# Expert layer of a float32 network: products with the weights' low parts moved to the end of each block, gates transposed together, and the context's first norm moved into the sums over V

## Chip, cores and metric

The kernel runs on one core of one Trainium2 chip. The metric is the time of one execution in microseconds of device time. The time before is 4041.46 us (the median of three runs). The profile below is of one more execution of the same program.

## What is computed

The network (d_model 1024, 512 tokens and a context of 256 tokens, all float32) has a first block of mixers, an expert layer, and a second block that works on the tokens together with the context. The change lies in the expert layer and where it meets the second block:

```python
def peer_ffn(xn, w_q, sub_keys, expert_u, expert_v):
    qh = (x2 @ w_q).reshape(t, PEER_HEADS, 2, PEER_QDIM // 2)
    scores = jnp.einsum('thcd,hckd->thck', qh, sub_keys, ...)
    sv, si = lax.top_k(scores, PEER_TOPK)
    ...
    cv, ci = lax.top_k(cand.reshape(...), PEER_TOPK)
    experts = (i1 * PEER_NKEYS + i2).reshape(t, PEER_HEADS * PEER_TOPK)
    gates = jax.nn.softmax(cv, axis=-1).reshape(...)
    # each token, for its 128 experts out of 16384:
    act = jax.nn.gelu(einsum('tkd,td->tk', expert_u[eb], xb))
    return einsum('tk,tkd->td', act * gb, expert_v[eb])
```

## The kernel before

**Float32 products.** A float32 operand is split into a high part and the rest (`split`, and `wload` for weights). `wload` loads 128x1024 raw weights (`wr`, three buffers, L194), ACT copies the high part `wh` (L142), and DVE subtracts to get the low part `wl` (L199). `mm3` then issues three matmuls for one product: L204 high by high, L205 and L206 with one low part each. `tt` is DVE's two-operand operation (L145), `stt` its operation with a scalar in between (L148), `copy` ACT's copy (L142), `transpose` a matmul with the identity (L236).

**The expert layer** (`peer`) treats the first 128 tokens apart from the other 384. For the 384, all 16384 experts are computed densely. `peer_h` makes H = gelu(U x) in 128 blocks of 128 experts, with 8 `mm3` (24 matmuls with 384 columns) to a block. In H, L204 and L205 use `wh` (L205 with x's low part) and L206 uses `wl`. A pair of blocks is written to the DRAM tensor `Hd` (L976). `peer_select` (on DVE) finds the 128 experts of each token, makes their gates and transposes both into three tiles `pi` (copies at L892 and L908). `peer_g` makes from them, by comparison with `iota` (`oa`, `ob`, then `ob` scaled by ACT) and 96 groups of 4 products (L995, 8 matmul records in the trace), a matrix G of gates which is zero wherever a token did not choose an expert, and writes it to `Gd` (L999). `peer_v` then sums over V. For each of its 128 blocks it needs V's block (`wh`, `wl`), H times G (`pa`, loaded as a pair of blocks from `Hd` at L1120 into one of two buffers, multiplied in place by `pg`, the loaded G, L1114) and the split of that product (`ph` by ACT, `pl` by DVE). A block is 18 matmuls with 512 columns into six accumulators. In V, L204 is ph by vh, L205 ph by vl (which needs `wl`), L206 pl by vh (which needs `pl`), three by three.

**The sparse path** handles the other 128 tokens: POOL gathers each token's rows of U (L915) and DVE takes the dot products (L931). In V's time POOL gathers rows of V, and PE sums them in groups of 8 small matmuls (L956, weights `sw`).

**Behind V** the sums are copied out (`py`, L1146), transposed (L236) and added to x; the squares of x are summed (`nsq`, `na`), and a matmul with ones (L267) begins x's norm. The stage `ctx0` starts with the context's norm (`norm`: for each of 8 slices `nt` on DVE, `xh` on ACT, `xl` on DVE, all 128x256) and projections of the context, 24 matmuls with 256 columns each; beside them a table of modulations is made (`mods`, L1175, weights `mw` from `wmod`).

**What sets the order.** Each engine executes its queue in order. The queues are what the scheduler of the tile framework makes of the program's order and of its own estimates, and the program's order comes from `interleave`, which runs several generators as lanes; each `yield busy, gap` tells it how far that lane's clock moves. H is the spare lane during selection and G, so where it yields decides where the other lanes' work may come between. A transfer is issued from SP's queue, in order too.

Of the kernel before, what the change touches and what calls it, by code (L numbers as in the profile page):

```python
# [23 lines left out]
CTX = 256  # L24
# [8 lines left out]
TS = 128  # L33
TD = SEQ - TS
# [8 lines left out]
def flat(t):  # L43
    return t.rearrange("p a b -> p (a b)")
# [61 lines left out]
class Net:  # L106
# [95 lines left out]
    def mm3(s, out, ah, al, bh, bl, start, stop):  # L202
        mm = s.nc.tensor.matmul
        mm(out, ah, bh, start=start, stop=False)  # L204
        mm(out, ah, bl, start=False, stop=False)  # L205
        mm(out, al, bh, start=False, stop=stop)  # L206

    def proj(s, w, xh, xl, nk, T, k0=0):

# [617 lines left out]
    def peer_select(s, p, sc, iota, iT, S):  # L827


        nc = s.nc  # L830
        cvs, late = [], []
        for tt in range(4):
# [60 lines left out]
                                          b[:, c * 128:(c + 1) * 128])  # L893
            late.append(transposed)
        late.pop(0)()
        for tt in range(4):
            ge = S["ge"] if tt == 0 else s.t(p, "pge", [128, 8, 16], 2)
            gm = s.t(p, "pgm", [128, 16], 2)[:, :8]
            s.tt(ge, cvs[tt], cvs[tt][:, :, 0:1].to_broadcast([128, 8, 16]), ALU.subtract)
            s.act(ge, ge, AF.Exp)  # L900
            yield 0.0, 1.0
            nc.vector.tensor_reduce(gm, ge, axis=AX.X, op=ALU.add)
            nc.vector.reciprocal(gm, gm)
            s.tt(ge, ge, gm[:, :, None].to_broadcast([128, 8, 16]), ALU.mult)
            if tt:
                b = s.bank()
                s.transpose(b[:, 0:128], flat(ge))
                nc.vector.tensor_copy(iT[2][:, (tt - 1) * 128:tt * 128], b[:, 0:128])  # L908
        S["gated"] = True

    def gather(s, S, table, idx):
# [50 lines left out]
    def peer_h(s, hp, xh, xl, Hd):  # L962

        for j in range(128):
            w = s.w()
            s.prime(min(2, 127 - j))
            ps = s.accb()[:, :TD]
            for k in range(8):
                s.mm3(ps, w[0][:, k, :], w[1][:, k, :], xh[:, k, TS:], xl[:, k, TS:], k == 0, k == 7)
                if k == 3:  # L970
                    yield 2.1, 0.0
            if j % 2 == 0:
                h = s.t(hp, "h", [128, 2, TD], 2)
            s.act(h[:, j % 2], ps, AF.Gelu_apprx_tanh)
            if j % 2:
                s.nc.sync.dma_start(Hd[j // 2], h)  # L976
            yield 2.1, 0.0
# [23 lines left out]
    def peer(s, x):  # L1001

        nc = s.nc
        with ExitStack() as st:
            dp = s.pool(st, "pd", space=bass.MemoryType.DRAM)
            Hd = dp.tile([64, 128, 2, TD], F32, name="Hd")
            Gd = dp.tile([TD // 32, 128, 128, 32], F32, name="Gd")
            keep = dp.tile([128, 8, SEQ], F32, name="keepx")  # L1010
            sp = s.pool(st, "sp")
            S = dict(n=0, rows=s.t(sp, "rows", [128, 128], 1, U32), rowsT=s.t(sp, "rowsT", [128, 128], 1, U32),
                     ge=s.t(sp, "sge", [128, 8, 16], 1), act=s.t(sp, "sact", [128, 128], 1),
                     aT=s.t(sp, "saT", [128, 128], 1), xt=s.t(sp, "sxt", [128, DM], 1),
                     w=[s.t(sp, f"sw{n}", [128, 4, 64], 1) for n in range(3)],
                     ring=[flat(x[:, 2 * n:2 * n + 2, :]) for n in range(4)]
                     + [s.t(sp, f"sr{n}", [128, DM], 1) for n in range(2)])
            for w in S["w"]:
                nc.gpsimd.memset(w, 0.0)
            v0 = s.pool(st, "pv0")  # L1020
            with ExitStack() as t:
                sv = s.peer_hg(t, x, Hd, Gd, S, keep)
            s.peer_v(v0, s.pool(st, "pv1"), x, Hd, Gd, S, sv, keep)

    def peer_hg(s, st, x, Hd, Gd, S, keep):
# [75 lines left out]
    def peer_v(s, p0, p1, x, Hd, Gd, S, sv, keep):  # L1101
# [8 lines left out]
        def dense():  # L1110
            js = 0
            for E in [2] + [6] * 21:
                g = s.t(p0 if js == 0 else p1, "pg", [128, TD // 32, E, 32], 1 if js == 0 else 2)
                nc.sync.dma_start(g, Gd[:, :, js:js + E, :].rearrange("b p j t -> p b j t"))  # L1114
                for e in range(E):
                    p, n = (p0, 2) if js % 4 < 2 else (p1, 2)
                    vh, vl = s.wload(s.I["V"][js], 8, p, n)
                    if js % 2 == 0:
                        a = s.t(p0 if js == 0 else p1, "pa", [128, 2, TD], 1 if js == 0 else 2)
                        nc.sync.dma_start(a, Hd[js // 2])  # L1120
                    av = a[:, js % 2].rearrange("p (b t) -> p b t", t=32)
                    s.tt(av, av, g[:, :, e, :], ALU.mult)
                    ah, al = s.t(p, "ph", [128, TD], n, F32R), s.t(p, "pl", [128, TD], n, F32R)
                    s.split(ah, al, a[:, js % 2])
                    vh, vl = flat(vh), flat(vl)
                    for h in range(2):
                        hh = slice(512 * h, 512 * h + 512)
                        for t in range(3):
                            tt = slice(128 * t, 128 * t + 128)
                            s.mm3(acc[t][h], ah[:, tt], al[:, tt], vh[:, hh], vl[:, hh], js == 0, js == 127)  # L1130
                    js += 1
                    yield 4.1, 0.0
            assert js == 128
# [3 lines left out]
            for k in range(8):  # L1137
                nc.sync.dma_start(x[:, k, :], keep[:, k, :])

        interleave([sv, reload(), dense()])  # L1140
        y = s.t(p1, "py", [128, 4, DM], 1)
        for h in range(2):
            hh = slice(512 * h, 512 * h + 512)
# [586 lines left out]
    def block2(s, x):  # L1730
# [3 lines left out]
        with ExitStack() as st:  # L1734
# [10 lines left out]
            xs, xf = [], []  # L1745
            with ExitStack() as t:
                s.mark("ctx0")
                xc, np_ = s.pool(t, "xc"), s.pool(t, "np")
                gain = s.small(np_, "nfin", 8)
                nc.sync.dma_start(gain, s.I["nfin"])  # L1750
                s.layer_consts(np_, 0)
                ch = s.norm(np_, xc, cx, mc[0][:, 8:16], CTX, mc[0][:, 0:8], s.early_r)
                with ExitStack() as t2:
                    s.mixers(t2, 0, CTX, xc, *ch, cx, True, [s.x_entry(np_, x, gain, xp, mx[0], xs),
                                                                    s.mods(s.pool(t2, "md"), 1, 0.5, 4)])
                mx.append(s.mod[1, 0])
                mc.append(s.mod[1, 1])
                for k in range(8):
                    nc.sync.dma_start(cx[:, k, :], s.I["ctxT"][:, k, :])
                s.mark("wo0c")  # L1760
                s.wo(np_, cx, CTX, mc[0], s.y)
                s.early_r = s.rstd(s.early, CTX)
            for i in range(2):
                if i:
                    s.mark("ctx1")
# [192 lines left out]
def network(st, tc, I):  # L1958
    s = Net(st, tc, I)
    s.mark("norm")  # L1960
    s.setup()
    x = s.pool(st, "xres").tile([128, 8, SEQ], F32, name="x")
    s.block1_mix(x)
    s.early = s.pool(st, "early")
    s.peer(x)
    s.block2(x)

# [17 lines left out]
```

## Time and profile before

| | us |
|---|---|
| runs shown: median, lowest, highest of 3 | 4041.46, 4036.75, 4047.43 |
| profiled execution: its own time | 4043.52 |
| profiled execution: span in the trace | 4041.8 |
| PE busy over the span | 3909.7 (97%) |
| DVE busy over the span | 2282.9 (56%) |
| ACT busy over the span | 1679.0 (42%) |
| granted TensorE clock, mean | 0.988 |

Times in the rows are microseconds from the start of the span. The stages that the change touches follow each other: selection with H beside it (about 790 to 1165), the rest of H with G (1165 to 1537), V (1537 to 2198), and the passage into `ctx0` (2198 to about 2220). A row of the view by stretch gives, per engine, busy time and the count of instructions. A row of a group gives busy time and mean duration, and behind the bar the time that the engine sat idle just before these instructions, with what ended it. PEld is the load of weights into TensorE, which overlaps the matmuls.

### The profile page before, as it was taken

What the parts mean: (1) busy time and instruction counts of PE and PEld (TensorE: products, weight loads), DVE (VectorE), ACT (ScalarE), POOL (GpSimd) and SP (SyncE); (2) the same over time, 40 slices, a digit from 0 to 9 for tenths busy, and PEclk for the clock granted to TensorE, in tenths of its full rate; (3) what the DMA queues carried; (4) which work ended last, traced back from release to release, by engine and by line L of the source; (5) the groups of instructions that cost most, each with busy time, mean ns of one, the idle gap of its engine ahead of it and who ended that gap; (6) DMA issues with size and microseconds to landing.
All of it is one profiled execution on the core that took longest, in us unless ns stands there. A gap on an engine that the chain in (4) does not pass through costs nothing.

```text
span 4041.8 us, 58180 instructions
## 1 busy us (share of the span) xinstructions
PE 3909.7 (97%) x22509; PEld 3272.3 (81%) x22509; DVE 2282.9 (56%) x4845; ACT 1679.0 (42%) x3136; POOL 328.0 (8%) x287
## 2 busy tenths in 40 slices
PE   8999999999999999999998999989999999989998
PEld 5878988789999995676777877878888888868887
DVE  7527544559999953344446847673222266664334
ACT  5335444433338872233333645552121245553222
POOL 0000000003234402322200000000000000000000
PEclk9999999999999999999999999999999999999999
DMA  5342123338789968888874751222212131122332
GB/s 196 106 151 77 34 92 106 114 109 282 255 278 367 382 221 310 279 299 291 293 273 162 253 200 48 67 65 68 63 63 65 58 128 63 48 89 80 98 94 84
DMA packets 218596, 637.63 MB, mean 158 GB/s; under 512 B 25552, under 2 KB 65360, under 8 KB 214736
## 3 DMA queue, kind: packets, MB, share of 16 engines
q1 hardware_dynamic: 181456, 499.69, 36.5%
q0 software_dynamic: 36864, 134.23, 9.1%
q8 instruction: 177, 2.90, 0.3%
q14 instruction: 99, 0.81, 0.1%
HBM read 575.12 MB, written 58.72 MB: 157 GB/s over the span
## 4 chain that ended last, share of the span: by engine, by line
PE 75%; DVE 13%; DMA 7%; issue 3%; ACT 2%; POOL 0%; SPq 0%; DVEq 0%; ACTq 0%; POOLq 0%
PE ac L204 18%; PE ac L205 18%; PE ac L206 18%; DMA pa<-Hd 6%; DVE wl L199 4%; PE bk L236 3%; PE bk L995 2%; PE po L1360 2%; PE bk L1175 1%; PE bk L204 1%; PE bk L205 1%; PE bk L206 1%; PE bk L561 1%; PE bk L555 1%; DVE pl L145 1%
## 5 line engine op out<-in xcount | busy, mean ns | idle before, releaser
L204 PE MATMUL ac<-xh,wh 128*128 128x512 f32 (+2 forms) x3608 | 1296.7, 361 | 12.9 <-ACT xh L142 4.4
L206 PE MATMUL ac<-xh,wl 128*128 128x512 f32 (+2 forms) x3608 | 1278.5, 355 | 6.1 <-DVE wl L199 5.8
L205 PE MATMUL ac<-xl,wh 128*128 128x512 f32 (+2 forms) x3608 | 1278.3, 355 | 0.8 <-DVE xl L148 0.6
L142 ACT ACTIVATE wh<-wr 128x1024 fp32r<-128x1024 f32 (+1 forms) x599 | 629.8, 1053 | 1555.7 <-PE ac L205 1109.3
L199 DVE TENSOR_TENSOR wl<-wr,wh 128x1024 fp32r<-128x1024 f32 (+1 forms) x599 | 727.6, 1216 | 558.6 <-ACT wh L142 520.6
L204 PEld LDWEIGHTS ac<-xh,wh 128*128 128x128 f32 x3608 | 682.2, 190 | 105.7 <-issue 17.0
L206 PEld LDWEIGHTS ac<-xh,wl 128*128 128x128 f32 x3608 | 681.9, 189 | 91.1 <-DVE wl L199 12.2
L205 PEld LDWEIGHTS ac<-xl,wh 128*128 128x128 f32 x3608 | 682.8, 190 | 78.3 <-issue 6.7
L145 DVE TENSOR_TENSOR pa<-pa,pg 128x384 f32<-128x384 f32 x128 | 66.2, 556 | 302.3 <-DMA pa<-Hd 291.0
L204 PE MATMUL bk<-wh,ph 128*128 128x512 f32 x512 | 202.0, 394 | 0.0
L206 PE MATMUL bk<-wh,pl 128*128 128x512 f32 x512 | 201.4, 393 | 0.0
L205 PE MATMUL bk<-wl,ph 128*128 128x512 f32 x512 | 201.2, 393 | 0.0
L204 PE MATMUL ac<-ah,wh 128*128 128x512 f32 (+1 forms) x528 | 186.1, 352 | 0.0
L205 PE MATMUL ac<-al,wh 128*128 128x512 f32 (+1 forms) x528 | 185.4, 351 | 0.0
L206 PE MATMUL ac<-ah,wl 128*128 128x512 f32 (+1 forms) x528 | 185.2, 351 | 0.0
L915 POOL DMA_INDIRECT x<-Ur,rows x86 | 123.2, 1433 | 399.5 <-DVE sc L825 212.4
L148 DVE SCALAR_TENSOR_TENSOR x<-ac,mod,x 128x512 f32<-128x512 f32 (+1 forms) x64 | 46.4, 726 | 188.2 <-PE ac L206 187.9
L142 ACT ACTIVATE ob<-ob,pi 128x128 f32<-128x128 f32 x384 | 125.1, 393 | 30.4 <-DVE ob L145 30.3
L142 ACT ACTIVATE ph<-pa 128x384 fp32r<-128x384 f32 x128 | 66.6, 521 | 169.1 <-issue 63.2
L915 POOL DMA_INDIRECT x<-V,rowsT x86 | 92.1, 1071 | 386.1 <-PE bk L956 363.0
L145 DVE TENSOR_TENSOR nt<-ac,nt 128x512 f32<-128x512 f32 (+1 forms) x44 | 29.9, 680 | 160.1 <-PE ac L206 159.8
L205 PE MATMUL ac<-wl,ph 128*128 128x512 f32 x256 | 103.5, 404 | 17.0 <-DVE wl L199 16.9
(453 smaller groups left out, 5843.1 us busy)
## 6 DMA issues: line engine op xcount, KB each, us to landing
wr<-win SPq DMA_DIRECT2D x151, 512.0 KB
wr<-U SPq DMA_DIRECT2D x128, 512.0 KB
wr<-V SPq DMA_DIRECT2D x128, 512.0 KB
mw<-wmod SPq DMA_DIRECT2D x96, 512.0 KB
Hd<-h SPq DMA_DIRECT2D x64, 384.0 KB
pa<-Hd SPq DMA_DIRECT2D x64, 384.0 KB
Gd<-gs SPq DMA_DIRECT2D x24, 1024.0 KB
pg<-Gd SPq DMA_DIRECT2D x21, 1152.0 KB
```

The source lines that it names most:

```text
L142: s.nc.scalar.activation(out, in_, AF.Copy, **kw)
L145: s.nc.vector.tensor_tensor(out, a, b, op=op)
L148: s.nc.vector.scalar_tensor_tensor(out, a, sc, b, op0=op0, op1=op1)
L199: (eng or nc.vector).tensor_tensor(lo[:, :nk, :], raw[:, :nk, :], r32(hi[:, :nk, :]), op=ALU.subtract)
L204: mm(out, ah, bh, start=start, stop=False)
L205: mm(out, ah, bl, start=False, stop=False)
L206: mm(out, al, bh, start=False, stop=stop)
L236: s.nc.tensor.transpose(out, in_, s.ident)
L555: mm(b[:, j], off[:, j], mi[:, j], start=True, stop=True)
L915: s.nc.gpsimd.indirect_dma_start(out=g, out_offset=None, in_=table, in_offset=bass.IndirectOffsetOnAxis(ap=idx, axis=0))
L995: nc.tensor.matmul(b[:, i * 128:(i + 1) * 128], a1[:, i], a2[:, i], start=True, stop=True)
L1360: mm(out[64 * h:64 * h + 64], heads[h][4][j], pt[:, 2 * (j - j0) + h, :], start=False, stop=j == nb - 1, skip_group_check=True)
```

## The change

1. A new `mm3s` for H issues the 16 products with `wh` of a block first and its 8 with `wl` behind them. The yield in the middle of a block moves behind the block.
2. In V a block's 18 products come as 6 ph·vh, 6 pl·vh, 6 ph·vl.
3. The gates of the three dense token blocks are kept in `pix` buffers; after all four are made the lane yields, then three transposes go into one bank and one 128x384 copy takes them out.
4. The context's first norm is a lane of V's `interleave` and its results lie in the pool `xc`, opened ahead of V on the right side of the memory, and closed behind the context's output projection.
5. `ctx_stack` is the stack that holds this pool.

```diff
+    def mm3s(s, out, w, xs, start=True, stop=True):
+        mm = s.nc.tensor.matmul
+        n = len(xs)
+        for k, (xh, xl) in enumerate(xs):
+            mm(out, w[0][:, k, :], xh, start=start and k == 0, stop=False)
+            mm(out, w[0][:, k, :], xl, start=False, stop=False)
+        for k, (xh, _) in enumerate(xs):
+            mm(out, w[1][:, k, :], xh, start=False, stop=stop and k == n - 1)
...
+        ges = []
         for tt in range(4):
-            ge = S["ge"] if tt == 0 else s.t(p, "pge", [128, 8, 16], 2)
+            ge = S["ge"] if tt == 0 else s.t(p, "pix", [128, 8, 16], 4)
             gm = s.t(p, "pgm", [128, 16], 2)[:, :8]
+            ges.append(ge)
...
-            if tt:
-                b = s.bank()
-                s.transpose(b[:, 0:128], flat(ge))
-                nc.vector.tensor_copy(iT[2][:, (tt - 1) * 128:tt * 128], b[:, 0:128])
+        yield 0.0, 6.0
+        b = s.bank()
+        for tt in range(1, 4):
+            s.transpose(b[:, (tt - 1) * 128:tt * 128], flat(ges[tt]))
+        nc.vector.tensor_copy(iT[2], b[:, :TD])
...
-            for k in range(8):
-                s.mm3(ps, w[0][:, k, :], w[1][:, k, :], xh[:, k, TS:], xl[:, k, TS:], k == 0, k == 7)
-                if k == 3:
-                    yield 2.1, 0.0
+            s.mm3s(ps, w, [(xh[:, k, TS:], xl[:, k, TS:]) for k in range(8)])
+            yield 2.1, 0.0
...
+            s.xc = s.ctx_stack.enter_context(s.tc.tile_pool(name="xc", bufs=1, side="right"))
             s.peer_v(v0, s.pool(st, "pv1"), x, Hd, Gd, S, sv, keep)
...
-                    for h in range(2):
-                        hh = slice(512 * h, 512 * h + 512)
-                        for t in range(3):
-                            tt = slice(128 * t, 128 * t + 128)
-                            s.mm3(acc[t][h], ah[:, tt], al[:, tt], vh[:, hh], vl[:, hh], js == 0, js == 127)
+                    for a_, v_, part in ((ah, vh, 0), (al, vh, 1), (ah, vl, 2)):
+                        for h in range(2):
+                            for t in range(3):
+                                nc.tensor.matmul(acc[t][h], a_[:, 128 * t:128 * t + 128],
+                                                 v_[:, 512 * h:512 * h + 512], start=js == 0 and part == 0,
+                                                 stop=js == 127 and part == 2)
...
-        interleave([sv, reload(), dense()])
+        s.ch, mc = [], s.mod[0, 1]
+        interleave([sv, reload(), s.norm_lane(p1, s.xc, s.cx, mc[:, 8:16], CTX, mc[:, 0:8], s.early_r, s.ch), dense()])
...
-                xc, np_ = s.pool(t, "xc"), s.pool(t, "np")
+                np_ = s.pool(t, "np")
...
-                ch = s.norm(np_, xc, cx, mc[0][:, 8:16], CTX, mc[0][:, 0:8], s.early_r)
...
-                    s.mixers(t2, 0, CTX, xc, *ch, cx, True, [s.x_entry(np_, x, gain, xp, mx[0], xs),
+                    s.mixers(t2, 0, CTX, s.xc, *s.ch, cx, True, [s.x_entry(np_, x, gain, xp, mx[0], xs),
```

The scheduler makes new queues of this. DVE's queue in the middle of V, first before (`pa` in place is the product with the loaded G, one row for both blocks of a pair; the blocks' `pl` and `wl` follow it):

```order
L145 TENSOR_TENSOR pa_15631<-pa_15631,pg_15490 128x384 x2
L145 TENSOR_TENSOR pl_15562<-pa_15558,ph_15561 128x384
L199 TENSOR_TENSOR wl_15555<-wr_15552,wh_15554 128x1024
L145 TENSOR_TENSOR pl_15591<-pa_15558,ph_15590 128x384
L199 TENSOR_TENSOR wl_15586<-wr_15583,wh_15585 128x1024
L953 COPY sw_1172_6418<-saT_6416 128x4
L145 TENSOR_TENSOR pa_15693<-pa_15693,pg_15685 128x384 x2
```

and in the change:

```order
L145 TENSOR_TENSOR pa_15994<-pa_15994,pg_15926 128x384
L199 TENSOR_TENSOR wl_15962<-wr_15959,wh_15961 128x1024
L145 TENSOR_TENSOR pl_15967<-pa_15934,ph_15966 128x384
L199 TENSOR_TENSOR wl_15991<-wr_15988,wh_15990 128x1024
L145 TENSOR_TENSOR pl_15998<-pa_15994,ph_15997 128x384
L145 TENSOR_TENSOR pa_16067<-pa_16067,pg_15926 128x384 x2
L199 TENSOR_TENSOR wl_16022<-wr_16019,wh_16021 128x1024
L145 TENSOR_TENSOR pl_16027<-pa_15994,ph_16026 128x384
```

Before, `pl` and `wl` of both blocks of a pair (here of `pa_15558`) stand behind the next pair's `pa` (`pa_15631`). In the change those of the pair's first block (`wl_15991`, `pl_15998` of `pa_15994`) stand ahead of the next pair's `pa_16067`, and only those of the second block behind it.

PE's queue behind V, first before (`py` are the sums, `na` the squares of x, `xh` and `xl` the context's normed parts, of which the first projection takes 24 matmuls):

```order
L236 MATMUL bk_18268<-ident,py_18215 128x128 x4
L236 MATMUL bk_18277<-ident,py_18215 128x128 x4
L236 MATMUL bk_18286<-ident,py_18215 128x128 x4
L267 MATMUL bk_18393<-na_18230,ones 128x512
L204 MATMUL ac_18424<-xh_18350,wh_13982 128x256
L205 MATMUL ac_18424<-xl_18351,wh_13982 128x256
```

and in the change (`L247` and `L278` are the former L236 and L267; between the two pieces lie two projections of 24 matmuls each):

```order
L247 MATMUL bk_18301<-ident,py_18248 128x128 x4
L204 MATMUL ac_18420<-xh_14010,wh_13981 128x256
L205 MATMUL ac_18420<-xl_14011,wh_13981 128x256
L247 MATMUL bk_18310<-ident,py_18248 128x128 x4
L206 MATMUL ac_18420<-xh_14010,wl_13982 128x256
L247 MATMUL bk_18319<-ident,py_18248 128x128 x4
...
L206 MATMUL ac_18459<-xh_14010,wl_13988 128x256
L278 MATMUL bk_18389<-na_18263,ones 128x512
L204 MATMUL ac_18501<-xh_14010,wh_18455 128x256
```

The two projections that followed the matmul with ones now precede it; behind it come two further ones and then the table of modulations. In DVE's queue two `wl` of these projections now stand between the last sums of `na`.

SP's queue at the end of H, first before (`wr<-U` are the loads of H's last blocks):

```order
L999 DMA Gd<-gs_13390 128x2048
L976 DMA Hd<-h_13578 128x768
L999 DMA Gd<-gs_13390 128x2048
L194 DMA wr_13752<-U 128x1024
L194 DMA wr_13980<-win 128x1024
L1114 DMA pg_14011<-Gd 128x12x64
```

and in the change:

```order
L194 DMA wr_13748<-U 128x1024
L194 DMA wr_13979<-win 128x1024
L988 DMA Hd<-h_13644 128x768
L1011 DMA Gd<-gs_13456 128x2048 x2
L194 DMA wr_13985<-win 128x1024
L1128 DMA pg_14016<-Gd 128x12x64
```

The last write of G stands behind the last load of U and the load of the next weights instead of ahead of them, so nearer to the end of H. On PE the last group of G stands two and a half blocks of H later, and G's groups come two at a time behind a whole block instead of one behind each half.

## Rows read from the trace of the kernel before

**Rows 1.** The page, the chain that ended last: shares by line.
```profile
PE ac L204 18%; PE ac L205 18%; PE ac L206 18%; DMA pa<-Hd 6%; DVE wl L199 4%; PE bk L236 3%; PE bk L995 2%; PE po L1360 2%; PE bk L1175 1%; PE bk L204 1%; PE bk L205 1%; PE bk L206 1%; PE bk L561 1%; PE bk L555 1%; DVE pl L145 1%
```

**Rows 2.** By stretch: length, busy PE, PEld, DVE, ACT, POOL; clock, DMA share, GB/s.
```profile
930.00:1165.00 235.00, 224.53 (x1250) 217.95 (x1248) 228.18 (x761) 74.35 (x103) 77.78 (x54) 0.99 0.83 277
...
1280.00:1400.00 120.00, 120.00 (x803) 120.00 (x802) 119.95 (x188) 96.26 (x241) 63.18 (x44) 1.00 1.00 396
...
1710.00:2062.00 352.00, 336.90 (x1576) 250.50 (x1568) 152.28 (x230) 109.90 (x143) 73.33 (x70) 0.99 0.81 293
...
2197.00:2210.00 13.00, 6.24 (x40) 4.89 (x38) 12.04 (x22) 6.48 (x11) 0.00 (x0) 0.81 0.02 2
```

**Rows 3.** Groups, 1710 to 2062: busy, mean ns, idle before, releaser.
```profile
L205 PE MATMUL ac<-wl,ph 128*128 128x512 f32 x144 | 58.3, 405 | 15.1 <-DVE wl L199 15.1
...
L145 DVE TENSOR_TENSOR pa<-pa,pg 128x384 f32<-128x384 f32 x71 | 36.6, 556 | 199.7 <-DMA pa<-Hd 192.7 <-issue 7.1
...
L205 PEld LDWEIGHTS ac<-wl,ph 128*128 128x128 f32 x144 | 27.3, 189 | 25.0 <-DVE wl L199 20.2
```

**Rows 4.** DVE and PE in order of time, one pair of V: start, duration, idle before.
```profile
1767.14 1.03 DVE L145 TENSOR_TENSOR pa<-pa,pg 128x384 f32<-128x384 f32 x2 [10.21 <-DMA pa<-Hd]
1768.09 0.55 DVE L145 TENSOR_TENSOR pl<-pa,ph 128x384 fp32r<-128x384 f32 x1
1768.55 1.22 DVE L199 TENSOR_TENSOR wl<-wr,wh 128x1024 fp32r<-128x1024 f32 x1
...
1769.83 0.50 PE L205 MATMUL ac<-wl,ph 128*128 128x512 f32 x1 [2.26 <-DVE wl L199]
...
1777.25 1.03 DVE L145 TENSOR_TENSOR pa<-pa,pg 128x384 f32<-128x384 f32 x2 [5.87 <-DMA pa<-Hd]
```

**Rows 5.** SP in the same stretch: the pair's load.
```profile
1770.27 0.33 SPq L1120 DMA_DIRECT2D pa<-Hd  x1
```

**Rows 6.** PE in order of time, from V's last product into `ctx0`.
```profile
2197.91 3.65 PE L236 MATMUL bk<-ident,py 128*128 128x128 f32 x32
2208.32 2.04 PE L267 MATMUL bk<-na,ones 128*128 128x512 f32 x2 [6.76 <-DVE na L145]
2209.38 1.20 PE L204 MATMUL ac<-xh,wh 128*128 128x256 f32 x1
...
2217.80 0.28 PE L206 MATMUL ac<-xh,wl 128*128 128x256 f32 x1
2219.11 0.39 PE L204 MATMUL ac<-xh,wh 128*128 128x256 f32 x1 [1.03 <-ACT za L1512]
```

**Rows 7.** The context's norm in its place of before: one of its two DVE groups.
```profile
L148 DVE SCALAR_TENSOR_TENSOR nt<-cx,mod,nr 128x256 f32<-128x256 f32 x8 | 3.5, 480 | 0.0
```

**Rows 8.** The chain of waits at V's start: the second pair's load.
```profile
1543.73 17.99 DMA pa<-Hd
```

**Rows 9.** Waits of an engine for another, 790 to 1165: us, times, longest.
```profile
PEld ac L206 <- DVE wl L199: 8.3, 15, 1.9
```

**Rows 10.** Groups, 1165 to 1524: the scaling of `ob`, and G's weights.
```profile
L142 ACT ACTIVATE ob<-ob,pi 128x128 f32<-128x128 f32 x384 | 125.1, 393 | 30.4 <-DVE ob L145 30.3
...
L995 PEld LDWEIGHTS bk<-ob,oa 128*128 128x128 f32 x768 | 100.7, 191 | 0.9 <-ACT ob L142 0.7
```

**Rows 11.** PE just behind a group of G, in order of time: H's products.
```profile
1284.78 0.42 PE L204 MATMUL ac<-xh,wh 128*128 128x384 f32 x1
1285.04 0.34 PE L205 MATMUL ac<-xl,wh 128*128 128x384 f32 x1
1285.21 0.34 PE L206 MATMUL ac<-xh,wl 128*128 128x384 f32 x1
```

**Rows 12.** SP, DVE and PE from G's last write to V's first product, in order of time.
```profile
1513.46 0.45 SPq L999 DMA_DIRECT2D Gd<-gs  x1
...
1524.45 0.56 DVE L145 TENSOR_TENSOR pa<-pa,pg 128x384 f32<-128x384 f32 x1 [2.11 <-DMA pg<-Gd]
...
1536.74 0.48 PE L204 MATMUL ac<-wh,ph 128*128 128x512 f32 x1
```

More of the change, by code (lines that the diff above doesn't have):

```diff
@@ L1762, in block2 @@
                 s.early_r = s.rstd(s.early, CTX)
+            s.ctx_stack.close()
             for i in range(2):
@@ L1963, in network @@
     s.block1_mix(x)
-    s.early = s.pool(st, "early")
+    s.early, s.ctx_stack = s.pool(st, "early"), st.enter_context(ExitStack())
     s.peer(x)
```

## The prediction

> **What bounds the kernel now.** I read the chain of waits first [rows 1]: PE's three products of the split arithmetic hold 54% of the span between them, and one transfer, the load of `pa`, another 6%. So the kernel is bound by PE nearly throughout, and an edit can gain only where PE stands still. Next I read busy times by stretch to see where that is [rows 2]. In 930 to 1165 (selection beside H) PE is busy for 224.53 of 235 us, and DVE for 228.18: two engines share the bound there. In 1280 to 1400 (H with G) both are full, 120.00 and 119.95 of 120. In the middle of V, 1710 to 2062, PE is busy for 336.90 of 352 us and DVE for only 152.28. Behind V, 2197 to 2210, PE works for 6.24 of 13 us, at a granted clock of 0.81 between its levels of 1.2 and 2.4 GHz, while DVE works for 12.04. Third, the groups of 1710 to 2062 tell what PE's 15.1 idle us there wait for: all 15.1 stand at L205 in the first accumulators, for `wl` [rows 3]. DVE is not short of time there. It sat 199.7 us in front of `pa`, and 192.7 of that ended with the load of `pa`.
>
> The order in time shows how these belong together [rows 4]. DVE takes its queue in order, so the `wl` of a block stands behind the next pair's `pa`: the wait for the load (10.21 us) ends at 1767.14, then come two `pa`, a `pl`, and only at 1768.55 the `wl`, 1.22 us long. PE's L205 starts at 1769.83 after a wait of 2.26, though the raw weights had nothing to do with `pa`. The next load leaves SP at 1770.27, when the pair's `pl` have freed a buffer [rows 5], and `pa` is used at 1777.25, 6.98 us later [rows 4]. That is a loop: 3.1 us of DVE, then a load. By the count of pairs in the stretch it takes 352 / 36 = 9.8 us a pair, while PE's work is 336.90 / 36 = 9.4.
>
> **The change, part by part.**
>
> *V's products, and what DVE's new queue makes of them.* Now PE needs `wl` at the second product of a block; in the change it needs `pl` at the seventh and `wl` at the thirteenth. The queue moves too: `wl` and `pl` of a pair's first block stand ahead of the next pair's `pa` in about three pairs of four (in the fourth, half of the `pa` comes first), and only the second block's stay behind it. So a late load no longer stops the first block. For the second block its `wl` ends 1.03 + 1.22 = 2.3 us behind the start of `pa` and is wanted twelve products in, over 2 us after the block began. The number of products, weight loads and vector operations stays the same. The gain lies between nothing (the loop of 3.1 us and a load stays the bound, and what PE no longer waits for at L205 it waits for at the start of a block) and 25 us (PE's weight loads sat idle for 25.0 us at that place, which takes in what pipelined ends hide [rows 3]). I take three quarters of PE's 15.1: **-11 us**. What is late next is `ph` of the next pair, since it needs the load itself.
>
> *The passage into ctx0.* Now the transposes (begun 2197.91, 3.65 us) end at about 2201.6; PE waits 6.76 us for DVE's last sum of squares, runs the matmul with ones at 2208.32, and two projections of 48 products from 2209.38 to 2217.80, on parts that DVE and ACT make at the same time [rows 6]. In the change these two projections have their operands long before and run among and behind the transposes. At the 8.4 us that they took, slow start and waits included, they end at about 2210. DVE gets two `wl`, 2 x 1.22 = 2.4 us [rows 4], between the last sums, so the matmul with ones comes at 2208.32 + 2.4 = 2210.8 and its duration to the next matmul is 2209.38 - 2208.32 = 1.1. PE is then at 2211.9 where it was at 2217.9 before, so 6.0 us are gained; of the 1.03 us that it stood before the third projection I expect the rest, as its weights are ready. **-7 us**, between 0 (the modulation table's loads, which cannot start earlier, take the time back) and -10 (6.76 + 1.03 + the slow clock's part).
>
> *The norm in its new place.* It is 16 DVE operations of about 0.48 us, 7.7 us by the row [rows 7], and 8 on ACT. They come ahead of the second pair's `pa`, whose load lasts 17.99 us at V's start [rows 8], with DVE idle for most of it and PE busy with the sparse sums: **0**. Without that cover it would delay the first `pa` products by up to 7.7 us, once.
>
> *H and selection.* The products with `wl` come 16 products into a block, not 3. PE's weight loads waited 8.3 us for `wl` in 790 to 1165 [rows 9]. But DVE is 97% busy in most of that, and none of its work goes except two small copies of gates; what PE gains it meets again where it waits for selection's results. **-3 us**, between -8 and +5 (G's start now waits for one copy of all gates).
>
> *G's groups in pairs.* A change from G to H costs PE one slow step: 1284.78 to 1285.04 is 0.26 us against 0.17 for the next [rows 11]. With 48 changes instead of 96, 48 x 0.09 = 4.3 us at most; half of it, as DVE is full there as well: **-2 us**.
>
> *G's last write.* It stood at 1513.46; the loaded G was used at 1524.45 and V's first product ran at 1536.74 [rows 12]. The last group of G moves back by two and a half blocks of H, each 24 products at 0.17, so 24 x 0.17 x 2.5 = 10.2 us. That puts the first `pa` at 1534.7, then `ph`, so just ahead of V's first product: **+1 us**, between 0 and +6.
>
> The **sum** is -11 - 7 - 3 - 2 + 1 = -22 us. The profiled execution took 4043.52 us, 1.7 over its span, and lies 2.1 above the median of the runs shown; on that median it gives 4041.46 - 22 = **4019.5 us**.
>
> **Rivals.**
>
> *V runs at PE's pace.* If the stalls go altogether, V gives 25 us, the passage 10 and H 5: about 4001. For it: PE's lag behind DVE shrinks, so `ph` (two buffers to a pool, freed by PE) is made earlier, and the loads with it. Against it: DVE waits for the load in every pair, whatever PE does. A load of `pa` is 384 KB and took 6.98 us from issue to use [rows 4, 5]. The Trainium skill, DMA: Bandwidth & Descriptors, in its section on the anatomy of one DMA, fits 2.0 us plus the bytes at 436 GB/s, an estimate of 2.9 us for this load (the fit is for transfers issued by GpSimd, which this one is not). By that the loop would be 6.0 us a pair and V bound by PE alone, and this rival would be the forecast. The trace does not agree: its load is more than twice that, as loads of weights share the queues at 0.81 of the engines' time [rows 2].
>
> *The loop holds V.* The wait moves from `wl` to `ph`, V gains 0 to 3, and the passage and the small terms are left: about 4030. For it: the loop's 9.8 us a pair is longer than PE's 9.4, and its terms hardly change. Against it: part of that loop is PE itself, through the buffers of `ph`.
>
> *G in pairs starves PE.* Between pairs of G, DVE and ACT must make two `oa` and two `ob`, with two buffers of each, while before they made one in half the time. ACT scales four slices of `ob` at 0.393 us for a group [rows 10]; if the second group of each pair waits for half of its scaling, 48 x 0.79 = 38 us are lost and the time is about 4041.5 - 20 + 38 = 4059, slower than before. It decides from 0.75 us a pair. For it: DVE has no slack at 119.95 of 120 and ACT is busy for 96.26 [rows 2]. Against it: until now only 0.9 us was spent waiting for `ob` [rows 10], and both buffers can fill during 24 products of H.
>
> *The change does not do what it says.* The new queues show the products, `wl` and the norm where the edits put them, so I give this nothing.
>
> **How the numbers follow.** A measurement of this kernel can tell about 0.3%, 12 us, from no change. The forecast, -13 to -30, has a chance of 0.55; V at PE's pace 0.20; the loop that holds V 0.17, with times on both sides of 12 us under the median but mostly within; G in pairs 0.08, of which a little falls within 0.3%. So faster 0.79, same 0.14, slower 0.07. The range goes down to 3998 (V at PE's pace and a little more from H) and up to 4036 (the loop holds V and one of the small terms costs instead of gaining), which leaves out the slow rival and about as much at the two edges.
>
> **What would show it.** In the middle of V, idle time before L205 for `wl` near zero, PE's share of 352 us up by some 11, and DVE still waiting for `pa` in each pair. Behind V, no idle stretch of 6 us before the matmul with ones, the clock not below 0.9, and the norm's `nt` between 1537 and 1565. In H, no waits for `wl` and still full DVE. Wrong would be: new idle time of PE before the first products of V's blocks as long as the old waits; waits of G's matmuls for `ob` above 20 us in all; or V's first product later than 1540 while H ends no later.

## The result, and the profile after

The change is slower: 4065.59 us (median of 6 runs, 4062.51 to 4069.94) against 4039.11 us for the kernel before on the same chips, a ratio of 1.0067 (95% interval 1.0055 to 1.0079). The forecast was 4019.5, in a range up to 4036. The profiled execution spans 4068.1 us.

Where the time went can be read from marks on PE. From V's first product to its last, 660.9 us became 687.7 (1536.7 to 2197.7 before, 1543.1 to 2230.8 after): **+27**. V begins 6.3 us later, of which 2.1 already lay ahead of selection, where nothing was changed. From V's last product to the end of PE's work, 1830.8 became 1824.1: **-7**. The same stretches as in [rows 2], after the change (length, busy PE, PEld, DVE, ACT, POOL; clock, DMA share, GB/s):

```profile
930.00:1165.00 235.00, 223.45 (x1252) 221.21 (x1251) 228.43 (x766) 78.20 (x105) 70.98 (x53) 0.98 0.81 277
...
1280.00:1400.00 120.00, 119.58 (x787) 117.93 (x785) 117.35 (x181) 98.04 (x239) 60.87 (x41) 1.00 0.99 389
...
1710.00:2062.00 352.00, 321.05 (x1477) 235.87 (x1476) 141.13 (x214) 100.71 (x132) 83.30 (x68) 0.96 0.75 270
...
2230.00:2243.00 13.00, 10.39 (x86) 9.83 (x84) 12.94 (x20) 8.08 (x12) 0.00 (x0) 1.00 0.04 12
```

The third row is the finding: in the middle of V PE is busy for 321.05 of 352 us where it had been for 336.90, it gets through 1477 records of matmuls where it had 1576, at a granted clock of 0.96, and the transfers move less too, 270 GB/s against 293. The last row is the passage behind V, in which PE now works for 10.39 of 13 us against 6.24, as intended.

Over the whole of V (the change, then before, each from its first product to its last) the count of records is the same but for one:

```profile
1543.06:2230.77 687.71, 644.79 (x2816) 455.02 (x2816) 281.89 (x433) 202.41 (x266) 141.31 (x122) 0.97 0.76 269
...
1536.74:2197.67 660.93, 638.22 (x2817) 450.39 (x2816) 277.01 (x417) 198.21 (x260) 129.67 (x122) 0.99 0.79 280
```

So 20 of the 27 us are idle time of PE (42.9 us against 22.7), and 7 are the same products taking longer, at a granted clock of 0.97 against 0.99.

What PE waits for in V, by groups of 1710 to 2062 (busy, mean ns, idle before, releaser), to set against [rows 3]:

```profile
L1144 PE MATMUL ac<-wh,pl 128*128 128x512 f32 x134 | 56.0, 418 | 31.0 <-DVE pl L145 30.8
...
L145 DVE TENSOR_TENSOR pa<-pa,pg 128x384 f32<-128x384 f32 x66 | 34.9, 556 | 212.1 <-DMA pa<-Hd 212.1
```

The waits for `wl` are gone, 15.1 us of them, and 31.0 us of waits for `pl` have come in their place. DVE stands longer in front of `pa` too, 212.1 us against 199.7, with fewer products with G done (66 instead of 71). One such wait in order of time (SP's issues, POOL's gathers, DVE, then PE; start, duration, idle before):

```profile
1794.36 0.33 SPq L194 DMA_DIRECT2D wr<-V  x1
1795.30 0.38 SPq L1128 DMA_DIRECT2D pg<-Gd  x1
1796.43 0.58 SPq L194 DMA_DIRECT2D wr<-V  x1
1797.11 0.39 SPq L1134 DMA_DIRECT2D pa<-Hd  x1
...
1793.43 1.72 POOL L929 DMA_INDIRECT sr<-V,rowsT  x1 [15.47 <-PE bk L970]
1795.45 1.76 POOL L929 DMA_INDIRECT sr<-V,rowsT  x1 [0.30 <-issue]
1797.52 1.31 POOL L929 DMA_INDIRECT x<-V,rowsT  x1 [0.30 <-issue]
1799.13 0.94 POOL L929 DMA_INDIRECT x<-V,rowsT  x1 [0.30 <-issue]
...
1797.93 0.55 DVE L145 TENSOR_TENSOR pl<-pa,ph 128x384 fp32r<-128x384 f32 x1
1810.89 1.03 DVE L145 TENSOR_TENSOR pa<-pa,pg 128x384 f32<-128x384 f32 x2 [12.41 <-DMA pa<-Hd]
1811.83 1.22 DVE L199 TENSOR_TENSOR wl<-wr,wh 128x1024 fp32r<-128x1024 f32 x1
1812.97 0.55 DVE L145 TENSOR_TENSOR pl<-pa,ph 128x384 fp32r<-128x384 f32 x1
...
1806.82 0.61 PE L1144 MATMUL bk<-wh,ph 128*128 128x512 f32 x2
1813.58 0.79 PE L1144 MATMUL ac<-wh,pl 128*128 128x512 f32 x1 [6.15 <-DVE pl L145]
```

Within six microseconds G's 1152 KB, two blocks of raw weights, four gathers of 512 KB each and `pa` are asked for together, and `pa` is used 13.8 us after its issue. PE has gone through the block's six ph·vh by 1807 and stands until 1813.58, because the `pl` that it wants next lies on DVE behind that `pa`. The same constellation returns every sixth pair, five times between 1790 and 2075, with loads of `pa` of 12.9 to 14.0 us. Each time PE then waits for 5.5 to 6.4 us (24 of the 31.0 us above are four of these waits), and during each of these waits the granted clock falls to the lower of its two levels, 1.2 GHz, for 6.8 to 10.2 us, in which products come 0.43 us apart instead of 0.22. For the wait shown, at a clock of 0.50:

```profile
1811.00:1817.50 6.50, 3.92 (x9) 3.14 (x10) 2.60 (x5) 2.91 (x4) 0.00 (x0) 0.50 0.41 145
```

Before, the four gathers that go with such a load of G came behind `pa`:

```profile
1844.00 0.38 SPq L1114 DMA_DIRECT2D pg<-Gd  x1
1845.61 0.33 SPq L194 DMA_DIRECT2D wr<-V  x1
1846.07 0.34 SPq L1120 DMA_DIRECT2D pa<-Hd  x1
...
1848.63 0.94 POOL L915 DMA_INDIRECT sr<-V,rowsT  x1 [16.14 <-PE bk L956]
...
1853.52 1.03 DVE L145 TENSOR_TENSOR pa<-pa,pg 128x384 f32<-128x384 f32 x2 [6.33 <-DMA pa<-Hd]
```

Here the load takes 7.4 us.

### The profile page after: what moved, and what is told of

The parts are those of the page before. It is cut to its first block, busy times and chain, and to the rows that moved or that the text cites. A ratio compares the mean times of both kernels' runs of the same rounds, so it can differ in the third digit from the quotient of the medians.

```text
span 4068.1 us, 58069 instructions
## 1 busy us (share of the span) xinstructions
PE 3917.3 (96%) x22509; PEld 3280.6 (81%) x22509; DVE 2281.3 (56%) x4843; ACT 1692.4 (42%) x3136; POOL 335.8 (8%) x287
## 4 chain that ended last, share of the span: by engine, by line
PE 79%; DVE 8%; DMA 8%; issue 2%; ACT 2%; POOL 0%; SPq 0%; DVEq 0%; ACTq 0%; POOLq 0%
PE ac L204 15%; PE ac L205 15%; PE ac L206 15%; DMA pa<-Hd 6%; PE bk L1144 4%; PE ac L214 3%; PE ac L215 3%; PE ac L217 3%; PE bk L247 3%; DVE wl L199 2%; PE ac L1144 2%; PE bk L1007 2%; PE po L1377 2%; PE bk L1192 1%; PE bk L572 1%
## 5 line engine op out<-in xcount | busy, mean ns | idle before, releaser
L204 PE MATMUL ac<-xh,wh 128*128 128x512 f32 (+1 forms) x2584 | 942.9, 366 | 10.5 <-ACT xh L142 4.1
L205 PE MATMUL ac<-xl,wh 128*128 128x512 f32 (+1 forms) x2584 | 933.3, 362 | 0.2
L206 PE MATMUL ac<-xh,wl 128*128 128x512 f32 (+1 forms) x2584 | 930.5, 361 | 1.5 <-DVE wl L199 1.5
L206 PEld LDWEIGHTS ac<-xh,wl 128*128 128x128 f32 x2584 | 488.6, 189 | 84.0 <-issue 8.1
L205 PEld LDWEIGHTS ac<-xl,wh 128*128 128x128 f32 x2584 | 489.3, 190 | 76.7 <-issue 7.2
L214 PE MATMUL ac<-xh,wh 128*128 128x384 f32 x1024 | 353.4, 345 | 4.3 <-ACT h L136 4.3
L215 PE MATMUL ac<-xl,wh 128*128 128x384 f32 x1024 | 349.3, 341 | 0.0
L217 PE MATMUL ac<-xh,wl 128*128 128x384 f32 x1024 | 201.2, 338 | 0.0
L205 PE MATMUL ac<-al,wh 128*128 128x512 f32 (+1 forms) x528 | 185.4, 351 | 0.0
L217 PEld LDWEIGHTS ac<-xh,wl 128*128 128x128 f32 x1024 | 182.3, 190 | 0.4 <-DVE wl L199 0.4
L1144 PE MATMUL bk<-wh,pl 128*128 128x512 f32 x512 | 163.7, 400 | 0.0
L1144 PE MATMUL bk<-wl,ph 128*128 128x512 f32 x512 | 162.9, 399 | 0.0
L1144 PE MATMUL bk<-wh,ph 128*128 128x512 f32 x512 | 159.3, 392 | 0.0
```

The costliest lines, as they stand in the source:

```text
L214: mm(out, w[0][:, k, :], xh, start=start and k == 0, stop=False)
L215: mm(out, w[0][:, k, :], xl, start=False, stop=False)
L217: mm(out, w[1][:, k, :], xh, start=False, stop=stop and k == n - 1)
L1144: nc.tensor.matmul(acc[t][h], a_[:, 128 * t:128 * t + 128], v_[:, 512 * h:512 * h + 512], start=js == 0 and part == 0, stop=js == 127 and ...
```

## Experiments

Each result is the median, with the ratio to the kernel before run beside it and its 95% interval; "V" is the time from V's first product to its last in the profiled execution. Kernels that leave V as it was gave V between 652 and 663 us, so that a difference of 10 in V from a single profile says little.

### Which part costs

Four kernels undo or keep whole parts of the diff: `V_undone` is the change with the loop over `mm3` put back in V; `V_only`, `N_only` (the norm) and `HG` (H's order and the gates) are the kernel before with those hunks alone.

> The change with V's 18 products again three by three; gates, H and the norm's new place stay. Theory A (V's new order alone costs the time: PE wants pl at a block's 7th product while pl of a pair's second block stands behind the next pair's load of pa, and that load got longer): V, first to last product, falls from the change's 688 us back to 661 +-5, and the whole is about 4037, 2 under before (H and G +5, passage behind V -7). Theory B (the norm's lane and its pool at V's start upset V): V stays above 680 and the whole above 4055. Theory C (V is late because G and its first load come late): V starts at 1543 as in the change and stays above 680.

> The kernel before with V's new product order alone. Theory A: V takes 685 to 692 us instead of 661, PE waits over 25 us for pl at the accumulators' first pl product, and the whole is about 4039 + 27 = 4066. Theories B and C: V stays at 661 +-5 and the whole within 10 us of before.

> The kernel before with the context's first norm in V's time alone. Theory A: V stays at 661 +-5, the passage behind V gains 6 to 7 us, the whole is about 4032. Theory B: V above 675, whole above 4050.

> The kernel before with the new H order and the gates transposed together alone. Theory A: H ends 4 to 6 us later (V's first product at 1541 to 1543 instead of 1536.5), V stays at 661 +-5, the whole is about 4044. Theory C: V above 675 and the whole above 4055. If the later end of H in the change was only scatter between executions, V starts at 1536 to 1538 and the whole is 4039 +-4.

| kernel | us | ratio | V |
|---|---|---|---|
| V_undone | 4037.72 | 0.9993 (0.9984 to 1.0002) | 662.6 |
| V_only | 4074.28 | 1.0083 (1.0068 to 1.0099) | 689.2 |
| N_only | 4031.62 | 0.9982 (0.9971 to 0.9992) | 653.2 |
| HG | 4047.11 | 1.0019 (1.0008 to 1.0029) | 661.8 |

Theory A holds and B and C fall: V's new product order alone costs all of it and more, the norm's move gains 7 us, and H with the gates costs 8. Two expectations were missed in detail: V of `N_only` came out below 661 +-5, by no more than the scatter just named, and in `HG` V's first product ran at 1539.2, ahead of the 1541 to 1543 of theory A. Two more split HG:

> The kernel before with the new order of H's products and its one yield behind a block alone. HG (with the gates as well) was 8 us over before. If H's order does it (G's groups two at a time, later): 4043 to 4048, with V's first product 2 to 3 us later. If the gates do it (G begins behind one late copy): 4036 to 4041.

> The kernel before with the gates transposed together alone. H_only was 1.6 over before within its interval, HG 8.5 over. If the one late copy of the gates does it: G's first product at 1234 to 1236 instead of 1228.5, the whole 4042 to 4047. If it takes both (G late, and in pairs): 4037 to 4041.

`H_only` came to 4040.74 (1.0007, 0.9997 to 1.0018) and `G_only` to 4038.35 (0.9997, 0.9986 to 1.0008): neither alone can be told from nothing. In HG G's last product runs at 1521.4, against 1511.4 (`H_only`) and 1517.4 (`G_only`) with one of the two and 1509.4 before. That the 8 us come from both together fits, but was not taken further.

### Is it the product order itself, or buffers

The first `-` line is `V_only`'s. `V_pa3` and `V_raw5` have `V_only`'s product order, `N_pa3` is `N_only` with a third buffer.

```diff
-for a_, v_, part in ((ah, vh, 0), (al, vh, 1), (ah, vl, 2)):
+for a_, v_, part in ((ah, vh, 0), (ah, vl, 1), (al, vh, 2)):   # V_hl_lh
-a = s.t(..., "pa", [128, 2, TD], 1 if js == 0 else 2)
+a = s.t(..., "pa", [128, 2, TD], 1 if js == 0 else 3)          # V_pa3, N_pa3
-vh, vl = s.wload(s.I["V"][js], 8, p, n)
+vh, vl = s.wload(..., raw=s.t(p1, "vr", [128, 8, 128], 5) if js > 1 else None)   # V_raw5
```

> The kernel before with V's 18 products as 6 ph x vh, 6 ph x vl, 6 pl x vh: only the last two sixes are exchanged against the change, so PE wants wl at a block's 7th product and pl at its 13th. DVE's queue then comes out nearly as before (next pair's pa, then pl, wl, pl, wl of the pair). Theory A1 (grouping the products does no harm by itself; the cost comes from the DVE queue that the scheduler made for the change's order, with wl ahead of pl and a pair's first block ahead of the next pa): V takes 640 to 661 us, the whole 4018 to 4039. Theory A2 (the grouping itself costs, since the lower parts are wanted together late in the block or accumulators are visited in turn): V stays at 685 to 692, the whole at 4066 to 4075.

> V_only (V's new order alone) with three buffers for pa instead of two. Theory L (V's pace is the loop of DVE's work on a pair and the load of the next pa into one of two buffers): V falls from 689 to below 665, DVE's wait for pa falls from 336 us to below 150, the whole to below 4050. Theory M (the loads as a whole are the pace, or the three buffers of raw weights are): V stays at 689 +-6, the whole above 4066.

> The kernel before with the context's norm moved and three buffers for pa. Theory L: V falls from 653 to 661 (with two buffers) to 625 to 640, as PE's own work is some 630, and the whole to 4000 to 4018. Theory M: V and the whole as with two buffers, 4032 +-5.

> V_only with five buffers for V's raw weights, of their own, instead of the three shared ones. Three buffers of pa changed nothing, as pa's load stands in SP's queue behind loads that wait for a raw buffer. Theory W (those waits make the loads come in one burst): V falls from 689 to below 665, the whole below 4050. Theory M (bandwidth, with gathers beside, whatever the buffers): V stays above 680.

| kernel | us | ratio | V |
|---|---|---|---|
| V_hl_lh | 4037.64 | 0.9998 (0.9988 to 1.0008) | 652.0 |
| V_pa3 | 4073.94 | 1.0087 (1.0073 to 1.0101) | 690.2 |
| N_pa3 | 4029.51 | 0.9977 (0.9966 to 0.9988) | 653.2 |
| V_raw5 | 4073.11 | 1.0078 (1.0059 to 1.0097) | 689.4 |

Grouping the products does no harm (A1), and no good either. Theories L and W both fall: neither a third buffer of `pa` nor five of raw weights changes V. So the loop on which the prediction was built, DVE's work and then a load into one of two buffers, is not by itself V's bound. More buffers of both kinds at once were not tried: in `V_pa3` SP still stands for 254.0 of 352 us in front of loads of raw weights until DVE has made a `wl`, in `V_raw5` for 245.2.

### Is it the gathers

`V_nog` and `B_nog` make each gather of a V row only in the first three of 32 steps (the later sums take rows that are already there, so the first 128 tokens are left wanting), `V_nog` on `V_only` and `B_nog` on the kernel before:

```diff
-gs = [s.gather(S, rows, ...) for g in range(4)]
+if t < 3:
+    gs = [s.gather(S, rows, ...) for g in range(4)]
+else:
+    gs = [S["ring"][(4 * t + g) % 6] for g in range(4)]
```

> V_only without POOL's gathers of V's rows behind the first three of 32 steps (the sums are made of rows already there, so the first 128 tokens' results are left wanting; the 2 MB a step that they load are gone). Theory K (the long loads of pa are its collisions with gathers and the load of G): DVE's wait for pa falls below 200 us and V to 630 to 645, no more than 5 above the same cut of the kernel before. Otherwise V stays 20 above it.

> The kernel before with the same cut (no gathers of V's rows behind the first three steps). Theory K: V takes 630 to 645 us against 661, as PE's own work sets it, and the order of the products no longer matters.

V falls to 601.3 and 601.4 us, the whole to 3984.87 (ratio 0.9867, 0.9851 to 0.9882) and 3987.1 (0.9872, 0.9853 to 0.9891). Without the gathers the order of the products no longer matters, and PE is busy in every microsecond of the middle of V. By stretch, `V_nog`:

```profile
1710.00:2062.00 352.00, 352.00 (x1668) 267.54 (x1667) 167.25 (x245) 124.70 (x157) 0.00 (x0) 1.00 0.62 211
```

So the cost of the new order arises only beside the gathers: they take 60 us of V before and 88 with the new order. Both times lie about 29 us under the 630 to 645 of theory K, because part of the 60 us lies elsewhere. At V's start (1545 to 1710, first before, then `B_nog`) PE gets through far fewer records in nearly the same busy time, which fits the way the gathers' sums come there, two or four records of `po` at a time instead of eight (third row, before); further on this turns out to be dear:

```profile
1545.00:1710.00 165.00, 159.29 (x616) 87.75 (x614) 52.50 (x84) 35.68 (x49) 54.07 (x50) 0.98 0.88 308
...
1545.00:1710.00 165.00, 161.45 (x774) 111.20 (x773) 76.78 (x116) 47.69 (x65) 4.67 (x4) 0.99 0.65 215
...
1601.17 1.04 PE L956 MATMUL po<-x,sw 128*32 128x512 f32 x2
```

How a load of `pa` depends on what goes beside it can be read from `V_only`, whose transfers have their landing times on record. In 1710 to 2062 the six loads that took over 12 us to land had 3600 to 3800 KB of other transfers beside them, the ten of 4.0 to 4.4 us less than 480 KB (an estimate that spreads each transfer's bytes evenly from its issue to its landing).

To see whether it is the gathers' coming four at once, `V_split` (on `V_only`) and `N_split` (on `N_only`) issue one gather with its matmuls at a time; a count of steps elsewhere goes from 8 to 32 with them, so that as many gathers as before fall ahead of V:

```diff
-gs = [s.gather(S, rows, ...) for g in range(4)]
+for g in range(4):
+    row = s.gather(S, rows, S["rowsT"][:, 32 * g + t:32 * g + t + 1])
...
+    yield 0.5, 3.75
```

> V_only with each sparse step of V cut in four: one gather (512 KB) and its matmuls at a time, a quarter of the distance apart; the bytes stay the same. Theory K (bursts of four gathers that fall on the loads of pa and G make the long loads): V falls from 689 to below 668 and the loads of pa over 12 us vanish; whole below 4053. If the amount of bytes is the limit: V stays at 680 to 692.

> The kernel before with the norm moved and the gathers one at a time. Theory K: V at most 653 (the value with the norm alone), perhaps 630 to 645 as PE's work sets it, the whole 4010 to 4030. If the amount of bytes is the limit, or small groups on PE cost what is won: 4030 to 4045.

Both failed as tests: 4152.18 (1.0276, 1.0260 to 1.0292) and 4144.39 (1.0256, 1.0240 to 1.0272). The reason is on PE. In `N_split`:

```profile
1804.60 1.04 PE L956 MATMUL po<-x,sw 128*32 128x512 f32 x2
1805.48 1.02 PE L956 MATMUL bk<-x,sw 128*32 128x512 f32 x2
```

and in the kernel before:

```profile
1765.21 1.06 PE L956 MATMUL po<-x,sw 128*32 128x512 f32 x8
```

Eight records of four gathers, which write four different groups of 32 partitions, take as long together as two of one gather do alone. Issued one by one they cost PE four times as much, so PE bounds V (771 us; it is busy for all of 1710 to 2062) and nothing is learned of the bursts.

### Is it the queue that the scheduler made

In the middle of V the change's own queue takes the `pa` of two pairs in six apart (11 of 33 in 1710 to 2062; before none): one block's product with G, then `wl` and `pl`, then the other block's. It keeps to six pairs, as the long loads do. Three kernels write V so that a pair's load and both its products with G come as a unit, and chain DVE's operations of V one behind the other by ordering edges without semaphores. `F_oldq_new` has the order of before (`pa` twice, then `pl`, `wl`, `pl`, `wl` of the pair before); `F_newq_old` and `F_newq_new` the change's order made regular (`pa` twice, `wl`, `pl` of the pair before's second block, `wl`, `pl` of the pair's first). The last word is the product order. The core of it:

```diff
+def next_(i):
+    if last:
+        s.tc.add_manual_dep(i.ins, last[0], NOSYNC, reason="queue")
+    last[:] = [i.ins.name]
...
+b = pair(k + 1) if k < 63 else None      # load of pa, both products with G
...
+for js in (2 * k + 1, 2 * k + 2):        # F_newq: second block of a, first of b
...
+    block(js, a if js % 2 else b, True)  # wl, then pl, then the 18 products
```

> The kernel before with V's new product order, and DVE's queue in V tied to the order that it had before (next pair's pa, then pl, wl, pl, wl of the pair); SP's queue comes out as before. Theory Q (the queue that the scheduler made for the new order costs the time): V takes 645 to 665 us, the whole 4022 to 4043. Theory P (PE's early want of pl costs it, whatever the queue): V stays at 680 to 692, the whole above 4058.

> The kernel before (products three by three) with DVE's queue in V tied to the change's order (next pair's pa, wl and pl of the second block, wl and pl of the next first block). Theory Q, queue alone: V 675 to 692, the whole 4052 to 4070. If the queue costs only together with the new product order, by bringing PE nearer to DVE and so moving the gathers: V 655 to 668.

> As F_newq_old (DVE and SP in V as tied there), but V's products in the change's new order; PE's order within a block is all that differs. Theory K (the loss is the times at which loads and gathers fall together in the scheduler's queue, where every third pair's pa is taken apart): no such lock here, V 635 to 660, the whole 4015 to 4042. Theory P (PE's early want of pl, which stands behind wl and the next pa, costs it): V 665 or more, the whole above 4045, with PE waiting over 25 us for pl.

| kernel | us | ratio | V |
|---|---|---|---|
| F_oldq_new | 4054.63 | 1.0039 (1.0025 to 1.0054) | 668.3 |
| F_newq_old | 4025.04 | 0.9955 (0.9939 to 0.9970) | 642.1 |
| F_newq_new | 4020.22 | 0.9953 (0.9935 to 0.9970) | 637.3 |

The last pair decides. DVE's and SP's queues are the same in both in the middle of V, and the products make no difference, so PE's wish for `pl` at the seventh product is not by itself the cause (theory P falls). With the same new products, three queues give 637, 668 and 689 us (the tied kernels change SP's order together with DVE's). In `F_newq_new`, by stretch, PE is never idle in the middle of V, and the transfers, all gathers among them, move 306 GB/s where the change moves 270, so the amount of bytes is not what held the change:

```profile
1710.00:2062.00 352.00, 352.00 (x1683) 265.14 (x1676) 165.57 (x245) 119.45 (x155) 78.25 (x70) 1.00 0.85 306
```

`F_oldq_new` missed its expectation by 12 us: the old queue takes back 21 of 28 us of V, not all. With everything of a pair behind the next `pa`, PE still waits for `pl` there, 12.0 us in its groups of 1710 to 2062:

```profile
L1154 PE MATMUL ac<-wh,pl 128*128 128x512 f32 x144 | 57.5, 399 | 12.0 <-DVE pl L1147 11.9
```

### A version that beats both

> F_newq_old (products three by three, DVE's queue tied to the new order by whole pairs) with the context's norm moved into V. If they add up: 4025 - 7 = 4018 +-4, below both kernels. If the norm's operations at V's start disturb the tied queue: 4025 or more.

4015.55 us, ratio 0.9941 (0.9922 to 0.9959), against 1.0067 for the change: the two add up. The regular queue with the new products and the norm's move was not tried together.

## Why the prediction was wrong

*V's products: the step that failed.* It said that V gains 11, between nothing and 25. Measured: it loses 27. The reading of the wait was right: the `wl` stood behind the next pair's load, the new queue took it out of there for the first block of a pair (ahead of all of the `pa` in two pairs of three; the prediction had three of four), and the waits at L205 went. What failed is the floor of that range: "nothing" is the case in which the loop of 3.1 us and a load stays the bound, at its length of before. For the second block only the `wl` was priced, as early enough; its `pl`, wanted at the seventh product, stands behind the next pair's `pa` as well, and there PE's 31.0 us of waits in 1710 to 2062 fell (15.1 before). A cost of the clock behind such waits was not in the sum either. Underneath lies one assumption: the lengths of the loads were taken as given. They are not: they depend on what else is asked for in the same microseconds. The gathers are released by PE's sparse groups, and the loads of G and the raw weights by DVE's progress, so shifting either can move them onto each other. In the change they fell together every sixth pair, and `pa` took 12.9 to 14.0 us. The kernels without gathers show that the loss needs the gathers; the tied queues show that it needs the queue that the scheduler happened to make, for in `F_newq_new` the same products with the same place of `pl` behind `pa` leave PE no wait at all in 1710 to 2062. Which feature of that queue brings the loads together, the `pa` taken apart or SP's order behind it, was not separated. SP's order alone does not do it: `V_raw5` issues `pa` right behind G's load, as the fast tied kernels do, and stays slow.

*The bound.* "DVE's work, then a load into one of two buffers" explained the times in the trace, but a third buffer changed nothing (`V_pa3`). A chain that fits every interval need not be the constraint; with a third buffer the load still stood behind raw weights' loads in SP's queue.

*The Trainium skill's fit* in DMA: Bandwidth & Descriptors (anatomy of one DMA), for transfers issued by GpSimd, gives an estimate of 2.9 us for such a load. The trace does not agree: in the middle of the change's V, 1710 to 2090, a load of `pa` takes between 4.0 and 14.0 us from issue to use, by what goes beside it, and the fit has no term for that. Without gathers (`B_nog`) the shortest there takes 2.8 us.

*The passage into ctx0.* -7 was forecast and -7 measured (V's last product to the end), and 4031.62 for `N_only` agrees. Over all profiles that stretch took 1821.9 to 1825.7 us in the six kernels with the norm moved and 1829.3 to 1833.5 in the fourteen without. Its steps fit, too:

```profile
2231.00 2.85 PE L247 MATMUL bk<-ident,py 128*128 128x128 f32 x24
...
2243.96 1.78 PE L278 MATMUL bk<-na,ones 128*128 128x512 f32 x2 [3.57 <-DVE na L145]
2244.75 1.20 PE L204 MATMUL ac<-xh,wh 128*128 128x256 f32 x1
2245.75 0.42 PE L205 MATMUL ac<-xl,wh 128*128 128x256 f32 x1
2245.97 0.41 PE L206 MATMUL ac<-xh,wl 128*128 128x256 f32 x1
```

The third projection starts 14 us behind V's last product (2230.8 to 2244.75) instead of 21 (2197.7 to 2219.11 [rows 6]). PE's wait before the matmul with ones shrank from 6.76 to 3.57, not to nothing, and the slow clock came back behind it: the projections' products stand 0.21 us apart there, against 0.12 in the two projections ahead of that wait, so the clock's part of the gain did not arrive. The norm's operations run from 1546 to 1568; V of `N_only` (653.2) and `V_undone` (662.6) lies within the scatter, so they cost nothing that can be seen, as forecast.

*H and selection, and G in pairs.* -3 and -2 were forecast; HG measured +8 (about +3 to +12 by its interval). In the change the waits for `wl` went (8.3 us of weight loads [rows 9], 1.4 after), but the stretch 930 to 1165 is as full of DVE as before, 228.43 us, and PE no busier: what was won at `wl` came back as other waits, 5.8 us of weight loads for ACT's `h` among them. Why both edits together cost 8 us stays open. The rival in which pairs of G starve PE did not come: the idle time before G's weight loads rose from 0.9 [rows 10] to 4.1 us. *G's last write*: +1 fits; V's first product waited 0.65 us, for `wh`, not for `pa`.

*The rivals.* "The loop holds V" and "V at PE's pace" were both built on loads of a fixed length, and none of the rivals let the loads themselves change. The slower case was put in the wrong stage.

## What to carry to other kernels

Where transfers take some 0.8 of the queues' time and several releasers issue them, as here, the length of a load can be a result of the order and not an input to it: look at what else is asked for within a few microseconds of the load that others wait for, and ask whether the edit shifts one releaser against another. A change of product order also changes what an estimating scheduler makes of the other engines' queues; test the two apart by tying the queue. Count with a wait of PE also what the granted clock does behind it: here 7 of V's 27 us are products that took longer. And before adding buffers, see whether the load behind the wait can be issued earlier at all, or stands behind something else in its queue.

## What was not expected of the hardware

Four small matmuls whose results go to different groups of 32 partitions ran side by side when issued next to each other (8 records in 1.06 us), and cost the same time each when issued apart (2 records in 1.04 us). The sum of all transfers in the middle of V was 270 GB/s in `V_only` and 306 in `F_newq_new`, with the same products and loads and other queues, while the stretch 1280 to 1400 of the kernel before moves 396.
